# Stores of gated activations move from the SyncE queue to the ScalarE queue in a one-core diffusion layer

## Chip, cores and metric

One core of a Trainium2 chip runs the whole kernel. The metric is the device time of one execution in microseconds, the median of three runs. TensorE is called PE below, its weight loads PEld, VectorE DVE, ScalarE ACT, GpSimd POOL and SyncE SP, as in the profile.

## What is computed

One layer of a hybrid backbone over 1024 latent tokens and 256 context tokens, width 1024, all in 32-bit floats:

```python
x   = x   + 0.5 * m2  * swiglu(modulate(rmsnorm(x),   m0,  m1),  w_ffn1_in, w_ffn1_out)
ctx = ctx + 0.5 * mc2 * swiglu(modulate(rmsnorm(ctx), mc0, mc1), w_ffn1_in, w_ffn1_out)
# one projection to q, k, v and the gates of a short convolution; latent queries
# attend to latent and context keys; both halves are joined
x   = x + m5 * (concat(rmsnorm(a), rmsnorm(s)) @ w_mix_out)
x   = x + 0.5 * m8 * swiglu(modulate(rmsnorm(x), m6, m7), w_ffn2_in, w_ffn2_out)
return rmsnorm(x)

def swiglu(h, w_in, w_out):              # hidden width 2816, 22 blocks of 128
    gate, up = split(h @ w_in, 2)
    return (silu(gate) * up) @ w_out
```

## The kernel before

Activations lie transposed, 128 features on the partitions, and latent tokens come in two halves of 512 columns (`L0`, `L1`); the context block is `CX` with 256. Every matrix product is made of three matmuls, from a high and a low part of both operands: `split` (L308) makes them by a cast on ACT and a subtraction on DVE (L309, L310).

Each SwiGLU is an object of class `FFN`. Its 22 hidden blocks ("units" below, index `f`) pass through two stages.

**First stage** (`phase_a`, L512, units 2 to 21; units 0 and 1 are made by plain products in the head). Latent tokens and output columns are each taken in two halves, and the 2x2 block product is made with seven products instead of eight, of 12 matmuls each. In time order they are M1, M6, M2, M5, M7, M4, M3; the first SwiGLU has two products for the context in between (cG, cU). ACT copies M1's bank out (`e1`, L528), after which M2 adds into the same bank, so M2's first matmul waits for that copy. ACT takes SiLU of M2's result (L531) and of M3's (L559), DVE makes the other sums and the two gating multiplications (L549, L579). At the odd unit of each pair POOL makes sums of gated blocks (L552, L554), and at the end of every unit one more (L583 or L585): these are the operands of a second seven-product scheme that the output projection uses. All of them are stored to DRAM:

- `store` (L349): for an odd unit P3 (the product of L549), P7 and P6 (POOL's sums of L552 and L554), then P2 (L579) and P4 (POOL, L583); for an even unit P1 (L579) and P5 (POOL, L585). That is seven stores of 256 KB in a pair of units.
- `spill` (L353) passes latent blocks on to `store`, and stores the context's gated block (128 KB, first SwiGLU only).

`prep` makes the weight operands of the next unit from raw tiles: `gA`, `S`, `sA`, `sB`, `uA`. At the end of a unit `load` (L460) asks for the raw tiles of unit `f+2` (L464, L465; three buffers with the tag `raw`, which the modulation weights share in the first SwiGLU). In that SwiGLU the modulation vectors are also computed beside the products (`ada_steps`, with a cast L152 on ACT and a subtraction L153 on DVE ahead of small matmuls L155, L156).

**Second stage** (`phase_b`, L670): steps named after `KINDS`, `P1` to `P4`, each of six blocks. `prep_b` loads the stored sums (`grt`, L651) and weights (`wr`, `res`, L614), splits them (`gst`, `wo`), and matmuls of L704 to L706 add into four banks, which L667 takes out. `pair0` (L361) loads four gated blocks of units 0 and 1 back, makes POOL's sums of them and stores these too.

**Order.** Each engine runs its own queue in order; an instruction at the head that waits holds everything behind it. The framework fixes each queue's order when the program is built: it keeps a model of when operands are ready, and gives an engine the earliest instruction of the program among those that it holds to be ready. All DMAs are issued from SP's queue, so loads and stores stand in one line there. Eight counters for landed DMAs are used in rotation, and a DMA waits until the one eight before it has landed.

Of the kernel before, what the change touches and what calls it, by code (L numbers as in the profile page):

```python
# [27 lines left out]
def layer_kernel(  # L28
# [18 lines left out]
    pe, act, dve, sp = nc.tensor, nc.scalar, nc.vector, nc.sync  # L47
# [286 lines left out]
    class FFN:  # L334
# [13 lines left out]

        def store(self, kind, p, t):  # L349
            p = (p - 1) % (NF // 2)  # L350
            sp.dma_start(self.gq[kind][p // 2][:, p % 2, :], t)

        def spill(self, f, b, t):  # L353
            if b is CX:
                sp.dma_start(self.gc[self.fs[f] // 2][:, self.fs[f] % 2, :], t)
            elif b is L0 and f % 2 == 0:
                sp.dma_start(self.g12, t)
            else:
                self.store("P3" if b is L0 else ("P1", "P2")[f % 2], f // 2, t)
# [661 lines left out]
    def side_b1(k, i):  # L1021
# [17 lines left out]
        elif k in ("P1", "P6", "P7"):  # L1039
            if k == "P1" and i == 0:  # L1040
                nc1[0] = norm_mod_steps(CX, 1, t2("rcx", [P, 256]))
            adv(nc1[0])
            if k == "P7" and i == 5:
                run(nc1[0])
                ctx_kv()
        elif k == "P4":
            if i == 0:
                nc1[0] = norm_mod_steps(L0, 1)
            adv(nc1[0], 2)
            if i == 5:  # L1050
                run(nc1[0])
                spill(L0, 0)

    F1.phase_b(side_b1)
    norm_mod(L1, 1)
    spill(L1, 1)


# [776 lines left out]
```

## Time and profile before

| What | Value |
|---|---|
| median of 3 runs | 2164.17 us (2163.52 to 2165.6) |
| time of the profiled execution | 2168.2 us |
| its span, first to last instruction | 2166.4 us |
| mean granted TensorE clock | 0.995 of full speed |
| first SwiGLU, first stage with its modulation work | about 111 to 636 us |
| second SwiGLU, first stage | about 1530 to 1922 us |
| second SwiGLU, second stage | about 1917 us to the end |

Busy time is the time in which an engine ran instructions; matmul ends are modelled and overlap, so the distance between starts tells PE's pace. A row of a timeline gives start, duration, engine (a q behind it: the queue itself, for issued DMAs), line, operation and tiles, and in brackets how long the engine was idle before it and what ended that. DMA issues are not part of an engine's busy time.

### The profile page before, as it was taken

How to read it: one execution, taken by the hardware profiler on the slowest of the kernel's cores; microseconds unless marked ns; L12 is line 12 of the kernel's file. 1: busy time of each engine (PE TensorE's matmuls, PEld its weight loads, DVE VectorE, ACT ScalarE, POOL GpSimd, SP SyncE). 2: the span in 40 equal slices, each digit the busy share in tenths (PEclk: the TensorE clock that was granted, in tenths of full speed). 3: DMA queues.
4: the chain of work that ended last, by engine and by line, in shares of the span. 5: the costliest groups of instructions: out<-in, count | busy, mean ns of one | idle time of the engine just before them, and what ended most of it. 6: DMA issues, size and time to landing. Idle time of an engine off the chain costs nothing.

```text
span 2166.4 us, 26536 instructions
## 1 busy us (share of the span) xinstructions
PE 2130.6 (98%) x10084; PEld 1711.8 (79%) x10084; DVE 1546.3 (71%) x2109; ACT 910.1 (42%) x1415; POOL 227.6 (11%) x158
## 2 busy tenths in 40 slices
PE   8999999999999999999999999999999999999998
PEld 4788788888889887887777777777788888877877
DVE  5887776666657867661898899876866666668754
ACT  4422322222335533442567777754422232234433
POOL 0001111101010110000100100001011111123001
PEclk9999999999999999999999999999999999999998
DMA  8043344545379756342211101142232322378642
GB/s 323 16 146 127 124 147 138 167 130 170 127 242 341 263 178 228 119 136 68 88 49 30 40 20 68 49 151 73 78 99 101 117 94 91 107 287 283 225 147 78
DMA packets 111824, 296.01 MB, mean 137 GB/s; under 512 B 10704, under 2 KB 17872, under 8 KB 108624
## 3 DMA queue, kind: packets, MB, share of 16 engines
q1 hardware_dynamic: 111696, 294.32, 40.1%
q8 instruction: 79, 1.29, 0.2%
q14 instruction: 49, 0.40, 0.1%
HBM read 235.29 MB, written 56.36 MB: 135 GB/s over the span
## 4 chain that ended last, share of the span: by engine, by line
PE 75%; DVE 6%; DMA 4%; issue 2%; ACT 2%; POOL 0%; DVEq 0%; SPq 0%; ACTq 0%; POOLq 0%
PE p L508 9%; PE p L510 9%; PE p L509 9%; PE po L704 6%; PE po L706 6%; PE po L705 6%; DMA wa<-in_ada_dram 3%; PE pT L1331 1%; PE pT L1330 1%; PE pmo L1110 1%; PE pmo L1111 1%; PE pmo L1112 1%; PE pvo L1354 1%; PE pvo L1355 1%; PE pvo L1353 1%
## 5 line engine op out<-in xcount | busy, mean ns | idle before, releaser
L704 PE MATMUL po<-gst,wo 128*128 128x512 f32 (+1 forms) x636 | 248.4, 391 | 3.4 <-DVE x L667 3.4
L706 PE MATMUL po<-gst,wo 128*128 128x512 f32 (+1 forms) x636 | 247.2, 389 | 4.0 <-DVE wo L310 4.0
L705 PE MATMUL po<-gst,wo 128*128 128x512 f32 (+1 forms) x636 | 247.3, 389 | 0.0
L309 ACT CAST gst<-grt 128x1024 fp32r<-128x1024 f32 (+1 forms) x95 | 88.9, 936 | 218.7 <-PE po L706 96.4
L310 DVE TENSOR_TENSOR gst<-grt,gst 128x1024 fp32r<-128x1024 f32 (+1 forms) x95 | 110.6, 1165 | 73.7 <-ACT gst L309 73.5
L706 PEld LDWEIGHTS po<-gst,wo 128*128 128x128 f32 x636 | 120.0, 189 | 31.9 <-DVE wo L310 5.1
L704 PEld LDWEIGHTS po<-gst,wo 128*128 128x128 f32 x636 | 120.1, 189 | 31.5 <-issue 2.7
L705 PEld LDWEIGHTS po<-gst,wo 128*128 128x128 f32 x636 | 120.2, 189 | 26.4
L142 DVE SCALAR_TENSOR_TENSOR acc<-wa,cs,acc 128x1024 f32<-128x1024 f32 x70 | 90.5, 1314 | 60.3 <-DMA wa<-in_ada_dram 60.3
L508 PE MATMUL p<-h0h,wgA 128*128 128x512 f32 x320 | 126.6, 396 | 0.2 <-ACT e1f L528 0.2
L509 PE MATMUL p<-h0l,wgA 128*128 128x512 f32 x320 | 126.4, 395 | 0.0
L510 PE MATMUL p<-h0h,wgA 128*128 128x512 f32 x320 | 126.4, 395 | 0.0
L1333 ACT ACTIVATE pexp<-pT 128x512 f32<-128x512 f32 x160 | 94.5, 598 | 66.6 <-PE pT L1331 35.1
L309 ACT CAST wsB<-s 128x512 fp32r<-128x512 f32 x80 | 48.5, 620 | 152.9 <-DVE s L495 83.0
L277 DVE TENSOR_TENSOR wm<-wr,wm 128x1024 fp32r<-128x1024 f32 x52 | 64.8, 1249 | 42.3 <-ACT wm L273 42.0
L310 DVE TENSOR_TENSOR wo<-wr,wo 128x1024 fp32r<-128x1024 f32 x72 | 83.3, 1163 | 15.2 <-ACT wo L309 15.2
L310 DVE TENSOR_TENSOR wsA<-s,wsA 128x512 fp32r<-128x512 f32 x80 | 51.8, 687 | 54.3 <-ACT wsA L309 54.3
L309 ACT CAST wo<-wr 128x1024 fp32r<-128x1024 f32 x72 | 70.3, 976 | 27.2 <-DVE wr L628 16.1
L309 ACT CAST wuA<-wr 128x1024 fp32r<-128x1024 f32 (+1 forms) x40 | 33.5, 838 | 107.6 <-issue 58.7
L309 ACT CAST wsA<-s 128x512 fp32r<-128x512 f32 x80 | 45.6, 618 | 68.9 <-PE p L510 63.1
L508 PEld LDWEIGHTS p<-h0h,wgA 128*128 128x128 f32 x320 | 60.1, 188 | 14.6 <-ACT e1f L528 0.6
L510 PEld LDWEIGHTS p<-h0h,wgA 128*128 128x128 f32 x320 | 60.1, 188 | 14.5
(1077 smaller groups left out, 5966.8 us busy)
## 6 DMA issues: line engine op xcount, KB each, us to landing
wr<-in_wo_dram SPq DMA_DIRECT2D x92, 512.0 KB, 4.7
wr<-in_wi_dram SPq DMA_DIRECT2D x88, 512.0 KB, 3.7
wa<-in_ada_dram SPq DMA_DIRECT2D x56, 512.0 KB, 3.6
wr<-in_wmi_dram SPq DMA_DIRECT2D x38, 512.0 KB, 3.6
grt<-g1P SPq DMA_DIRECT2D x35, 512.0 KB, 4.8
grt<-g2P SPq DMA_DIRECT2D x35, 512.0 KB, 6.0
g1P<-ev SPq DMA_DIRECT2D x35, 256.0 KB, 3.2
g2P<-ev SPq DMA_DIRECT2D x35, 256.0 KB, 2.0
```

What stands on the lines that cost most here:

```text
L142: dve.scalar_tensor_tensor(acc[:, i, :], w, cs[:, j, k:k + 1], acc[:, i, :], op0=ALU.mult, op1=ALU.add)
L277: dve.tensor_tensor(w[:, 1, :], r, w[:, 0, :].bitcast(F32), op=ALU.subtract)
L309: act.copy(hi, t)
L310: dve.tensor_tensor(lo, t, hi.bitcast(F32), op=ALU.subtract)
L508: pe.matmul(pt, w[:, 0, c:c + P], hi, start=(k == 0 and not more), stop=False, skip_group_check=more)
L509: pe.matmul(pt, w[:, 0, c:c + P], lo, start=False, stop=False, skip_group_check=more)
L510: pe.matmul(pt, w[:, 1, c:c + P], hi, start=False, stop=(k == 3), skip_group_check=more)
L704: pe.matmul(o, wh, hi, start=st, stop=False, skip_group_check=g)
L705: pe.matmul(o, wh, lo, start=False, stop=False, skip_group_check=g)
L706: pe.matmul(o, wl, hi, start=False, stop=end, skip_group_check=g)
L1110: pe.matmul(pt, wh, hi[:, k, :], start=(i == 0), stop=False)
L1333: act.activation(p, pt, AF.Exp)
```

## The change

`store` and the context branch of `spill` issue their DMA from ACT's queue instead of SP's. Nothing else is edited: the store of the first L0 block (`g12`), all loads, spills of the residual and output stores stay on SP. The framework makes the order of all queues anew.

```diff
         def store(self, kind, p, t):
             p = (p - 1) % (NF // 2)
-            sp.dma_start(self.gq[kind][p // 2][:, p % 2, :], t)
+            act.dma_start(self.gq[kind][p // 2][:, p % 2, :], t)
 
         def spill(self, f, b, t):
             if b is CX:
-                sp.dma_start(self.gc[self.fs[f] // 2][:, self.fs[f] % 2, :], t)
+                act.dma_start(self.gc[self.fs[f] // 2][:, self.fs[f] % 2, :], t)
```

## Rows read from the trace of the kernel before

**Rows 1.** The page, part 1: busy us (share of span) of each engine
```profile
PE 2130.6 (98%) x10084; PEld 1711.8 (79%) x10084; DVE 1546.3 (71%) x2109; ACT 910.1 (42%) x1415; POOL 227.6 (11%) x158
```
**Rows 2.** Busy time by stretches: second SwiGLU's first stage, then its second stage's start
```profile
1770.00:1905.00 135.00, 135.00 (x581) 108.94 (x581) 88.34 (x117) 39.61 (x63) 19.74 (x13) 1.00 0.29 100
1905.00:1960.00 55.00, 52.17 (x221) 40.90 (x220) 37.52 (x36) 16.54 (x18) 11.65 (x8) 1.00 0.91 329
```
**Rows 3.** PE's waits, 100 to 640 us: total, times, longest
```profile
PE pr L156 <- DVE alo L153: 2.1, 3, 0.8
...
PE p L508 <- ACT e1f L528: 0.2, 1, 0.2
```
**Rows 4.** PE's waits, 1525 to 1905 us
```profile
PE p L510 <- DVE wsA L310: 1.0, 1, 1.0
```
**Rows 5.** PE's waits, 1905 to 2000 us
```profile
PE po L706 <- DVE wo L310: 1.9, 2, 1.3
PE po L704 <- DVE x L667: 1.5, 2, 0.9
```
**Rows 6.** The stores of line L351: engine, op, count, duration ns min/median/max
```profile
L351 SPq DMA_DIRECT2D g2P<-ev x35: 319/320/339, 1567.2 to 1926.6; - x35
...
L351 SPq DMA_DIRECT2D g1P<-e1f x15: 319/327/1040, 137.6 to 630.1; - x15
```
**Rows 7.** Timeline of SP's queue, 1720 to 1734 us (an odd unit)
```profile
1723.70 2.08 SPq L351 DMA_DIRECT2D g2P<-ev  x2
1726.84 0.32 SPq L351 DMA_DIRECT2D g2P<-e1f  x1
1727.25 0.38 SPq L464 DMA_DIRECT2D wr<-in_wi_dram  x1
1728.53 0.32 SPq L351 DMA_DIRECT2D g2P<-ev  x1
1730.28 0.32 SPq L351 DMA_DIRECT2D g2P<-gt  x1
```
**Rows 8.** Timeline of SP's queue, 1701 to 1712 us (the even unit before it)
```profile
1704.73 0.33 SPq L464 DMA_DIRECT2D wr<-in_wi_dram  x1
...
1709.70 0.33 SPq L351 DMA_DIRECT2D g2P<-gt  x1
```
**Rows 9.** Timeline of ACT, 1720 to 1734 us
```profile
1724.58 1.06 ACT L309 CAST wgA<-wr 128x1024 fp32r<-128x1024 f32 x1 [2.13 <-PE p L510]
1725.53 0.63 ACT L559 ACTIVATE ev<-ev 128x512 f32<-128x512 f32 x1
1727.55 0.59 ACT L528 COPY ev<-p 128x512 f32<-128x512 f32 x1 [1.39 <-DMA g2P<-ev]
1733.03 0.60 ACT L531 ACTIVATE e1f<-p 128x512 f32<-128x512 f32 x1 [4.89 <-PE p L510]
```
**Rows 10.** Timeline of POOL, 1720 to 1734 us
```profile
1725.51 1.31 POOL L554 TENSOR_TENSOR e1f<-ev,e1f 128x512 f32<-128x512 f32 x1
1728.63 1.62 POOL L583 TENSOR_TENSOR gt<-e1f,ev 128x512 f32<-128x512 f32 x1 [1.82 <-issue]
```
**Rows 11.** Timeline of PE, 1729 to 1731 us: M2's first matmul
```profile
1729.98 0.40 PE L508 MATMUL p<-h0h,wgA 128*128 128x512 f32 x1
```
**Rows 12.** Chain that ended last, 1900 to 2000 us: start, us, what
```profile
1928.87 0.32 SPq L351
1929.24 0.43 SPq L614
...
1936.31 6.83 DMA resc<-in_wo_dram
...
1944.38 1.22 DVE wo L310
```
**Rows 13.** Timeline of POOL, 1936 to 1950 us: the last sum of the first pair
```profile
1941.21 2.17 POOL L374 TENSOR_TENSOR g<-g,g 128x512 f32<-128x512 f32 x1
```
**Rows 14.** Timeline of ACT, 1936 to 1950 us
```profile
1939.74 1.06 ACT L309 CAST gst<-grt 128x1024 fp32r<-128x1024 f32 x1 [14.25 <-DMA grt<-g2P]
```

## The prediction, as put on record before the result was known

> **What bounds the kernel now.** I read the page first, then the busy time by stretches, then what PE waited for, and last SP, ACT, POOL and PE side by side over one pair of units. PE is busy for 98% of the span, ACT for 42% [rows 1]. In the second SwiGLU's first stage PE has no gap in 135 us: 581 matmuls, one per 0.232 us, at full granted clock, while ACT runs 39.6 us of these 135 and the DMA engines are busy 0.29 of the time [rows 2]. That stage is bound by PE alone, so whatever the stores do there can't make it faster; it can only make it slower. What the change can win is PE's waits near the stores. There are few. In the first SwiGLU's first stage the larger ones are 2.1 us for a subtraction of the modulation work, and 0.2 us for the copy of M1's bank [rows 3]. In the second SwiGLU's first stage there is one wait of 1.0 us, at its very start [rows 4]. Where the second stage begins there are 1.9 us for weight splits and 1.5 us for the taking out of banks [rows 5]. Together 6.7 us, which is 0.3% of the time: the ceiling of every gain.
>
> **What is moved, and its price on ACT.** Counted from the code: seven stores in each of ten pairs of units and in two SwiGLUs make 140; units 0 and 1 add three for each SwiGLU, `pair0` four for each, the context 22. That is 176 stores. On SP an issue takes 0.32 us, the longest 1.04 [rows 6]. The trace shows no DMA on ACT, so these are the bounds there; I take 0.33, since a median of the same instruction is the nearest row. It is added work, so it can't be below nothing. 176 x 0.33 = 58 us on an engine with 2166 - 910 = 1256 us idle [rows 1]: hidden as long as no instruction behind a store has PE waiting for it.
>
> **Who has PE waiting.** One instruction of ACT does, in every unit: the copy L528 of M1's bank, for M2 adds into that bank. In the odd unit shown it runs from 1727.55 to 1728.14 [rows 9], and M2's first matmul starts at 1729.98 [rows 11]: 1.84 us to spare. The weight casts (`wgA` and the like) are made a whole unit, 84 x 0.232 = 19.5 us, ahead of use, and SiLU L531 comes 5.5 us after the copy. So up to 1.8 us of delay ahead of L528 is free, and each further microsecond costs one.
>
> **What the stores put ahead of it.** They wait for their data at the head of the queue. In the odd unit, SP issued P3 at 1723.70, P7 at 1723.70 + 2.08 - 0.32 = 1725.46, P6 at 1726.84, P2 at 1728.53 and P4 at 1730.28 [rows 7]; P6 comes as POOL's second sum ends at 1726.82, and P4 as its third ends at 1730.25 [rows 10]. The order of ACT's new queue isn't in the trace, but one row tells what the builder does with stores: the load L464, which in the even unit was issued at 1704.73 [rows 8], would have been due one unit later at about 1724.3, and stands behind P3, P7 and P6, at 1727.25 [rows 7]. So the builder thinks POOL's sums are ready earlier than they are, and lets them go first. I assume the same on ACT: P3, P7, P6, then SiLU L559, the cast `wgA`, and L528. Worked out: P6 leaves ACT at 1726.84 + 0.33 = 1727.17, L559 takes 0.63 (1727.80), `wgA` 1.06 (1728.86), L528 0.59 (1729.45) [rows 9]. That is 0.5 us ahead of M2 at 1729.98 [rows 11]. With P2 ahead of L528 as well (0.33 more) it is 0.2 us ahead. Cost: nothing, but most of the cover is used. Behind L528 there is none to hurry until L531 at 1733.03 [rows 9], by which P2 and P4 have long gone. In the first SwiGLU two context products lie around these steps; the one tight copy there is late already by 0.2 us [rows 3]. A store just ahead of each of these four waits [rows 3] would cost 4 x 0.33 = 1.3 us; that is the upper bound, nothing the lower, and I take nothing, since casts and copies there mostly stand in idle stretches of ACT.
>
> **What it frees on SP.** In the first stages a raw tile asked for at 1704.73 [rows 8] is cast at 1724.58 [rows 9], so 3 us more or less [rows 7] are worth nothing. At the end of the second SwiGLU's first stage they are. The chain that ended last runs there through the store P4, issued at 1928.87, the load right behind it at 1929.24, a load that lands after 1943, and the split `wo` at 1944.38, for which PE waits [rows 12]. With P3 to P4 gone from SP's queue these loads can leave up to 6 us earlier. Gain: nothing at the least (the stretch moves 329 GB/s with the DMA engines busy 0.91 of the time [rows 2], so an earlier start may only lengthen the transfers); all 3.4 us of [rows 5] at the most; I take 1.3, the longest of those waits, as it is the one to which this chain leads. [...]
>
> **`pair0`.** Its four stores wait for POOL's sums, the last until 1943.38 [rows 13]. On ACT they pass the casts of that stretch, the first of them at 1939.74 [rows 14]. If the builder puts them ahead of that cast they hold it for up to 1943.38 + 0.33 - 1939.74 = 3.97 us, and PE with it; if behind, nothing. I take nothing: on SP they stood behind loads for the steps that these casts serve. In the first SwiGLU the same four lie beside context steps without a PE wait.
>
> **The sum.** ACT's issues 0, copies 0, loads -1.3, `pair0` 0: -1.3 us on the profiled execution's own 2168.2 us (span 2166.4). The median of the runs, 2164.17, lies 4.0 us below that execution; the same step from it gives 2162.9 us.
>
> **The rivals.**
> - *A store waits for POOL ahead of the copy* (slower). If the builder puts P4 ahead of the next unit's L528, the copy starts at 1730.28 + 0.33 = 1730.61 and ends at 1731.20, 1.22 us after M2 was due [rows 7, 9, 11]. This decides as soon as P4 stands ahead of L528, wherever the rest stands. Nine odd units of the second SwiGLU have such a copy behind them: 11.0 us. In even units P5 is issued at 1709.70 [rows 8], the copy would end at 1710.62, and M2 is due at 1729.98 - 19.5 = 1710.5: 0.1 us each, 1 us for ten. So 12 us in the second SwiGLU; with as much in the first, 24. For it: the builder already hurries POOL's sums, and P4 stands earlier in the program than L528. Against it: P4 comes 2.7 us after the copy's start, more than the 1.3 to 1.6 us of one POOL sum [rows 10] by which the builder may be wrong. Time: 2164.2 + 12 = 2176 (to 2188 with both).
> - *Loads freed everywhere* (faster). All 6.7 us of PE's waits go: 2157.5. For it: the wait for `alo` hangs on modulation loads in the same queue. Against it: [rows 3, 4] name ACT and DVE, not a DMA, as what ended these waits.
> - *It does nothing*: the loads are held by the landing of earlier ones, and ACT hides the issues: 2164.2.
> - *The issue on ACT is dearer.* At 1.04 us [rows 6] P6 leaves ACT at 1727.88, and the copy ends at 1727.88 + 0.63 + 1.06 + 0.59 = 1730.16, 0.2 us late, nine times: +2 us. [...]
>
> **How the numbers follow.** A difference of 0.2% (4.3 us) is about what a measurement of this kernel can tell from no change. My forecast together with "does nothing" and "dearer issue": 0.56, from 2160.8 (all of [rows 5] won) to 2167.5. The store ahead of the copy: 0.32, from 2170 to 2188. Loads freed everywhere: 0.12. So faster 0.12, same 0.56, slower 0.32. The likeliest case gives 2162.9. The range starts at 2159.5, a little beyond the bound of 2160.8, and ends at 2178, where the first form of the slower rival is in and the second, with some 0.1 of the chance, is left out.
>
> **What would show it.** Right: ACT's queue shows 0.3 us issues, L528 in the odd units moves from 1.4 us of idle time to directly behind `wgA`, and M2 follows M1 and M6 without a gap; SP's loads of the second stage's start leave some 5 us earlier and the wait for `wo` is gone. Wrong, slower side: PE waits for "ACT L528" about nine times at 1.2 us, and ACT waits for POOL's `gt` ahead of L528. Wrong, faster side: the waits of [rows 3] are gone. If PE's waits change in stages that hold no store, such as attention, then it is the new order of the queues as a whole that moved the time, which none of these sums covers.

## The result, and the profile after

The changed kernel takes 2195.0 us (median of 4 runs, 2192.67 to 2196.87) beside 2164.89 us for the kernel before on the same chip: a ratio of 1.0133, interval 1.0119 to 1.0147. It is slower by 30 us, above the upper end of the forecast range. The profiled execution took 2192.67 us with a span of 2190.9 us, against 2166.4 us before: 24.5 us more. The other 5.6 us lie between the medians and the profiled executions, which took 3.3 us more than the median before and 2.3 us less after.

By the starts of matmuls, these 24.5 us divide as follows (microseconds). The first SwiGLU's first stage is counted to the first matmul of its context steps, its second stage to its last matmul; the second SwiGLU's first stage is counted to its own last matmul, and the rest of the second stage from there to its last.

| Stage | before | after | difference |
|---|---|---|---|
| first SwiGLU, first stage | 524.8 | 531.1 | +6.3 |
| first SwiGLU, context steps and second stage | 287.6 | 293.2 | +5.6 |
| attention and what lies around it | 607.1 | 606.3 | -0.8 |
| second SwiGLU, first stage | 394.2 | 407.8 | +13.6 |
| second SwiGLU, rest of the second stage | 233.5 | 233.0 | -0.5 |

One trace gives such a stage to within some 3 us only: the last row, 233.5 us before, was 236.7 us in the run with only the first SwiGLU's last two units on ACT, whose second SwiGLU stores from SP as before, and where the granted clock stood at 0.50 twice more, for 3.4 us each.

ACT's busy time hardly changed, since issues don't count in it, and PE stayed busy for 98% of a longer span [rows 1]. The page of the changed kernel, part 1:

```profile
PE 2136.7 (98%) x10084; PEld 1714.3 (78%) x10084; DVE 1528.0 (70%) x2109; ACT 908.2 (41%) x1415; POOL 222.6 (10%) x158
```

The same 135 us of the second SwiGLU's first stage by stretches (start:end, length, then busy time and instructions of PE, PEld, DVE, ACT and POOL, clock, DMA share, GB/s): 561 matmuls where there were 581 [rows 2], at full clock.

```profile
1770.00:1905.00 135.00, 131.19 (x561) 105.08 (x560) 81.93 (x113) 37.42 (x60) 18.95 (x13) 1.00 0.27 92
```

PE's waits in that stage, 1540 to 1935 us. Before, there was the last of these lines alone, with 1.0 us [rows 4]:

```profile
PE p L508 <- ACT ev L528: 6.4, 5, 1.3
PE p L508 <- ACT e1f L528: 5.1, 4, 1.3
PE p L510 <- DVE wsA L310: 1.5, 1, 1.5
```

Nine waits of 1.3 us for the copy L528, one behind each odd unit with a successor: the picture that the slower rival asked for. The timeline of ACT over one of them, 1741 to 1753 us, answers [rows 9]:

```profile
1741.66 2.09 ACTq L351 DMA_DIRECT2D g2P<-ev  x2
1744.81 0.33 ACTq L351 DMA_DIRECT2D g2P<-e1f  x1
1745.18 0.63 ACT L559 ACTIVATE ev<-ev 128x512 f32<-128x512 f32 x1 [4.78 <-POOL e1f L554]
1745.71 1.04 ACT L309 CAST wgA<-wr 128x1024 fp32r<-128x1024 f32 x1
1746.57 0.33 ACTq L351 DMA_DIRECT2D g2P<-ev  x1
1748.32 0.33 ACTq L351 DMA_DIRECT2D g2P<-gt  x1
1748.74 0.58 ACT L528 COPY ev<-p 128x512 f32<-128x512 f32 x1 [1.99 <-POOL gt L583]
1752.48 0.60 ACT L531 ACTIVATE e1f<-p 128x512 f32<-128x512 f32 x1 [3.16 <-PE p L510]
```

POOL's sum and PE's first matmul of M2 at the same place, from their timelines:

```profile
1746.67 1.62 POOL L583 TENSOR_TENSOR gt<-e1f,ev 128x512 f32<-128x512 f32 x1 [1.90 <-issue]
```

```profile
1749.38 0.50 PE L508 MATMUL p<-h0h,wgA 128*128 128x512 f32 x1 [1.29 <-ACT ev L528]
```

Read from the bottom: M2 waits for the copy, the copy stands behind the store P4 (`gt`) in ACT's queue, and P4 stands at its head until POOL's sum ends at 1748.29. M1's last matmul had started at 1744.90, so the copy's data had long been there. M2 starts 1.44 us later after M1 than it does behind an even unit; 9 x 1.44 = 13.0 us, and 0.5 us more at the stage's start (1.5 for `wsA` instead of 1.0) makes 13.5 of the 13.6 us. Behind an even unit the copy stands ahead of the store P5: in the unit before it ends at 1726.36, and M2 starts at 1728.37, 2.0 us later.

### The profile page after: what moved, and what is told of

It reads as the page before. It is cut to its first block, busy times and chain, and to the rows that moved or that the text cites. A ratio compares the mean times of both kernels' runs of the same rounds, so it can differ in the third digit from the quotient of the medians.

```text
span 2190.9 us, 26509 instructions
## 1 busy us (share of the span) xinstructions
PE 2136.7 (98%) x10084; PEld 1714.3 (78%) x10084; DVE 1528.0 (70%) x2109; ACT 908.2 (41%) x1415; POOL 222.6 (10%) x158
## 3 DMA queue, kind: packets, MB, share of 16 engines
q8 instruction: 79, 1.29, 0.2%
```

## The experiments

The runs of a group shared their runs of the kernel before; "ratio" is time over theirs, with its 95% interval. Stage times are from the traces, counted as in the table above. In these kernels `store` takes a queue as a last argument `q`; where a diff doesn't show that line, a store without it goes to ACT.

**P4 alone back on SP.**

```diff
-                        self.store("P4" if h else "P5", pi, t)
+                        self.store("P4" if h else "P5", pi, t, sp if h else act)
```

> The changed kernel with one store moved back: the odd units' P4 is issued from SP again, all others stay on ACT. Theory (P4 waits for POOL at the head of ACT's queue, ahead of the copy L528 for which M2 waits): the nine gaps of about 1.27 us of PE in the second SwiGLU's first stage go, that stage falls from 407.8 us to between 394 and 396, and the first SwiGLU's first stage, where few P4 stand ahead of a copy, from 531.1 to between 526 and 530; the second stages stay. Time 2195.0 - 12.6 - (1 to 5) = 2177 to 2182. Rival (it is the number of issues on ACT, or the new order of all queues, and not this one wait): the second SwiGLU's first stage stays above 404 us, and the time between 2190 and 2196.

2177.0 us, ratio 1.0054 (1.0039 to 1.0068). The second SwiGLU's first stage took 394.1 us, 0.1 less than before the change, without one wait for L528; the first SwiGLU's 527.3. One of the seven kinds of store carries the 13 us, although 20 of 176 issues left ACT.

**`pair0` alone back on SP.**

```diff
             for k, v in (("P5", t1), ("P7", b12), ("P6", b11), ("P4", b21)):
-                self.store(k, 0, v)
+                self.store(k, 0, v, sp)
```

> The changed kernel with the four stores of pair0 moved back to SP in both SwiGLUs. Theory (the 5.6 us that the first SwiGLU's second stage lost come from pair0's stores, which wait for POOL ahead of the casts of gst and wo on ACT): that stage falls from 231.8 us to about 226, the PE gap of 3.4 us at its start is gone, the clock there stays at its full level, the first stages keep 531 and 408 us; time about 2189. Rival (the loss comes from the order in which the loads and the last units' P4 stand, pair0 has no part in it): the stage stays at 231 to 232 us and the time at 2194 to 2196.

2191.1 us, ratio 1.0118 (1.0102 to 1.0135). The theory fell: context steps and second stage of the first SwiGLU still took 292.5 us (293.2 with the full change). The interval overlaps that of the full change (1.0119 to 1.0147), so the times alone don't show that `pair0` cost anything. The traces show a wait that went, where the second SwiGLU's second stage begins. PE's waits were, in the full change (1930 to 2025 us):

```profile
PE po L704 <- DVE x L667: 2.4, 1, 2.4
```

and with `pair0` on SP (1929 to 2025 us):

```profile
PE po L704 <- DVE x L667: 0.3, 1, 0.3
```

The wait of 2.4 us was followed by 3.4 us at a granted clock of 0.50, from 1979.1 us, which the run with `pair0` on SP does not have there. Both traces still took 640.8 us for the second SwiGLU's two stages as counted above: at the end of the second run the clock stood at 0.50 for 3.4 us twice more than in the full change.

The chain that ended last in the full change, 1944 to 1985 us, tells what the wait hung on (start, us, what):

```profile
1962.25 6.16 DMA g2P<-g
1968.43 5.15 DMA grt<-g2P
1973.68 1.06 ACT gst L309
1978.26 0.67 DVE x L667
1979.07 0.72 PE po L704
```

The first line is a store of `pair0`, issued by ACT. It landed at 1968.41, and SP issued the load `grt` 0.02 us later: both have the same one of the eight counters, and the load comes next on it after the store. Of this trace's 669 DMAs none was issued before the one ahead of it on its counter had landed. The load brings other blocks than those that `pair0` stores. The other three stores of `pair0` each held one of SP's issues in the same way (1963.67, 1967.20 and 1970.31, within 0.06 us of the landing); in the kernel before and in the run with `pair0` on SP no issue followed one of them so closely. So stores that had left SP's queue still held SP's issues here.

**P4, P5 and `pair0` back on SP**, the edits of both runs together, and P5 as well.

```diff
-                        self.store("P4" if h else "P5", pi, t)
+                        self.store("P4" if h else "P5", pi, t, sp)
```

> The changed kernel with P4, P5 and pair0 moved back to SP; P1, P2, P3, P7, P6 and the context's blocks stay on ACT, 104 issues. Theory (only stores that wait for POOL ahead of a copy or a cast cost): first stages at about 525 and 395 us, first SwiGLU's second stage at 226 to 227, second SwiGLU's second stage keeps its small gain; time 2164 to 2169. Rival (each issue on ACT costs a share of the 30 us): 104 of 176 issues are left, so 2195 - 30 x 72/176 = 2183.

2173.4 us, ratio 1.0038 (1.0023 to 1.0053), between the two expectations. The first stages took 525.4 and 395.0 us, as the theory said; the first SwiGLU's context and second stage stayed at 295.1.

**All on ACT, P4 behind the copy.** P4 is issued in the program after the next unit's SiLU of M2 (`pair0` from SP).

```diff
-                        self.store("P4" if h else "P5", pi, t)
+                        if h and f < NF - 1:
+                            late = pi, t
+                        else:
+                            self.store("P4" if h else "P5", pi, t)
...
                         act.activation(e2, p1, AF.Silu)
+                        if h == 0 and f > f0:
+                            self.store("P4", *late)
```

> The changed kernel with P4 still on ACT, but written in the program behind the next unit's SiLU of M2, so that it stands behind the copy L528 in ACT's queue; pair0 from SP. The number of issues on ACT is that of the changed kernel less eight. Theory (the place in the queue decides, not the engine or the number of issues): second SwiGLU's first stage 394 to 396 us, first SwiGLU's 526 to 530, time 2165 to 2176. Rival (ACT can't carry these issues, wherever they stand): second SwiGLU's first stage over 404 us, time over 2188.

2173.3 us, ratio 1.0035 (1.0017 to 1.0052); the second SwiGLU's first stage took 394.0 us. ACT at an odd unit, 1730 to 1740 us of this kernel:

```profile
1734.52 1.03 ACT L309 CAST wgA<-wr 128x1024 fp32r<-128x1024 f32 x1
1735.37 0.33 ACTq L351 DMA_DIRECT2D g2P<-ev  x1
1735.80 0.59 ACT L528 COPY ev<-p 128x512 f32<-128x512 f32 x1 [0.25 <-DMA g2P<-ev]
1737.12 0.33 ACTq L351 DMA_DIRECT2D g2P<-gt  x1
```

The copy ends at 1736.39, and M2 starts without a wait at 1736.74: 0.35 us to spare. This is the order that the prediction had assumed, with P2 ahead of the copy, for which it had worked out 0.2 us.

**Five kinds of store in the second SwiGLU only, and four of them.**

```diff
-            sp.dma_start(self.gq[kind][p // 2][:, p % 2, :], t)
+            (q or (act if self.which in (2,) and kind in ('P3', 'P7', 'P6', 'P2', 'P4') else sp)).dma_start(self.gq[kind][p // 2][:, p % 2, :], t)
```

> The kernel before, with only the second SwiGLU's odd-unit stores P3, P7, P6, P2 and P4 issued from ACT: 50 issues instead of 176; the first SwiGLU, P1, P5 and pair0 are untouched. In ACT's queue P2 and P4 stand ahead of the copy L528. Theory (P4 at the head of ACT's queue waits for POOL and holds the copy): the second SwiGLU's first stage is 407 to 409 us, as with all 176 issues; its second stage 234 to 237; the first SwiGLU as before. Time 2164.2 + 13 - (1 to 3) = 2174 to 2177. Rival (the loss grows with the number of issues): 13.6 x 50/70 = 9.7 us and less than 404 us for the stage; or none, if the even units' P5 did it: 394.

> As the run with five stores, but P2, which DVE makes and which waits for no POOL sum, is issued from SP again. P4 stays on ACT; with one issue less ahead of it the builder puts it behind the copy L528. Theory (only the place of P4 against the copy counts): the second SwiGLU's first stage falls to 394 to 395 us, no PE wait for L528 is left, and the time is 2160 to 2164. Rival (P4 on ACT costs in itself, or P2 has a price of its own of 0.3 us in ten units): 404 us and more, or 394 + 3.

With five: 2178.0 us, ratio 1.0059 (1.0041 to 1.0077), the stage 407.9 us, as long as with all the stores. With four, P2 being the one left out: 2164.5 us, ratio 0.9993 (0.9981 to 1.0005), the stage 393.8 us. PE's waits with five, 1540 to 1905 us (with four there is none):

```profile
PE p L508 <- ACT ev L528: 6.4, 5, 1.3
PE p L508 <- ACT e1f L528: 5.1, 4, 1.3
```

P4 is on ACT in both. With four it stands behind the copy (timeline of ACT, 1715 to 1730 us):

```profile
1726.80 0.59 ACT L528 COPY ev<-p 128x512 f32<-128x512 f32 x1
1728.25 0.33 ACTq L351 DMA_DIRECT2D g2P<-gt  x1
```

One store, which waits for no POOL sum, changes where the builder puts P4, and that is worth 14 us. P2 itself ahead of the copy costs nothing: it stands there in the runs with P4 on SP and with P4 late as well, where the stage took 394.1 and 394.0 us.

**All kinds in the second SwiGLU only, P4 late**: the edit of the fourth run, with `act if self.which else sp` in `store`.

> All stores of the second SwiGLU's first stage from ACT, with P4 written in the program behind the next unit's SiLU of M2, so that it stands behind the copy; pair0 and the whole first SwiGLU from SP as in the kernel before. Theory (the gain of the freed SP queue is confined to the second SwiGLU's second stage, 2.5 to 3.4 us there when neither P4 nor pair0 holds ACT, against 1.2 in the changed kernel): first stage 394, second stage 234 to 235.5, time 2160.5 to 2162. Rival (the gain came from the changed first SwiGLU and is not here): 2164.

2162.3 us, ratio 0.9985 (0.9976 to 0.9995): a little faster than the kernel before. Of the waits of [rows 5] 0.3 us was left. The second stage, which the expectation counts from its own first matmul, took 236.6 us against 237.8, where 234 to 235.5 was expected; the trace shows why. After the wait of 2.1 us for `wo` near the end, which both kernels have, the granted clock stood at 0.50 for 3.4 us twice before the last matmul, and in the kernel before not at all. Up to that wait the rest of the second stage took 214.9 us against 218.7.

**Only the last pair of units of the second SwiGLU.**

```diff
-            sp.dma_start(self.gq[kind][p // 2][:, p % 2, :], t)
+            (q or (act if self.which == 2 and self.tail else sp)).dma_start(self.gq[kind][p // 2][:, p % 2, :], t)
...
+                self.tail = f >= NF - 2
                 pi, h = divmod(f, 2)
```

> The kernel before, with only the seven stores of the last pair of units of the second SwiGLU issued from ACT; pair0 and all else from SP. No copy L528 follows the last P4. Theory (the gain of the change is that the loads of the second stage no longer stand behind stores that wait for POOL, at this one place): second SwiGLU's first stage 394, its second stage 234 to 236 us against 237.8, time 2161 to 2163. Rival (the gain needs a queue free of stores through the whole first stage, for loads made early): second stage 237.5 to 238, time 2164 to 2165.

2163.1 us, ratio 0.9981 (0.9971 to 0.9991), the lowest ratio of all, with seven stores moved (its interval overlaps that of the run before). The second stage took 231.5 us from its first matmul against 237.8, more gain than the 2 to 4 us expected; 3.4 us less at a clock of 0.50, some 1.7 us, are part of it. PE's waits from 1905 us to the end; the kernel before had 4.0, 2.6 and 0.6 us under these names:

```profile
PE po L708 <- DVE wo L310: 2.1, 1, 2.1
PE po L706 <- DVE x L669: 1.1, 2, 0.8
PE rb L211 <- DVE rs L204: 0.6, 1, 0.6
```

**What cost 5.6 us in the first SwiGLU's second stage.** PE's waits came to 5.3 us against 1.7; some 1.7 us more are the clock, which fell after the longest (see the last section). The waits in the full change, 640 to 930 us; the kernel before had the second and third line alone (0.9 and 0.8 us):

```profile
PE po L704 <- DVE x_c L667: 3.4, 1, 3.4
PE pv L292 <- ACT wv L273: 0.9, 1, 0.9
PE po L704 <- DVE x L667: 0.7, 1, 0.7
PE po L704 <- DVE rs L204: 0.3, 1, 0.3
```

In DVE's queue the taking out of the context's banks (`x_c`) stands behind weight subtractions that wait for loads. The timeline of DVE in the full change, 704 to 711 us (before, that line ran at 694.72, as the context steps ended; here they ended at 700.50):

```profile
704.59 1.22 DVE L310 TENSOR_TENSOR wo<-wr,wo 128x1024 fp32r<-128x1024 f32 x1
706.33 1.23 DVE L626 TENSOR_TENSOR res<-wr,res 128x1024 f32<-128x1024 f32 x1 [0.53 <-DMA res<-in_wo_dram]
707.47 3.22 DVE L667 SCALAR_TENSOR_TENSOR x_c<-po,mod,x_c 128x256 f32<-128x256 f32 x8
```

Two things had changed besides: SP issued three of the four 1 MB loads of the residual `x` ahead of the context steps instead of one (a second came 0.8 us after their start), and DVE's queue had two more subtractions L628 ahead of the reciprocal `rs`. Three runs, each built on the one with P4, P5 and `pair0` on SP, took these apart: two loads of `x` held, three held, and, with three held, the two subtractions on POOL. The first diff is of the run with two held, the second of the last.

```diff
             if i in (12, 16):
+                g = F1.pg[i][:, 0, 0:1].bitcast(F32)
+                pool.tensor_tensor(L1.x[i // 16][:, 0, 0:1], g, g, op=ALU.add)
                 half_x(L1, xt_d, 512, i // 16)
...
-                dve.tensor_tensor(r, r, R, op=ALU.subtract)
+                e = pool if k == "P6" and u >= 4 and self.cx else dve
+                e.tensor_tensor(r, r, R, op=ALU.subtract)
```

> As the run with P4, P5 and pair0 on SP, with one thing more: the last two 1 MB loads of the residual x in the first SwiGLU are held back until the context steps 12 and 16 (a one-column addition on POOL writes into their target first), so that they stand again where the kernel before issued them, some 28 and 39 us after the first context step, instead of one of them 4 us ahead of it. Theory (SP, freed of the stores, issues this 1 MB ahead of the weight blocks of wo, the DMA engines are busy for over 0.9 of the time there, and the blocks, the DVE work on them and the taking out of the context's banks behind it come late): context stage and second stage together fall from 295.2 us to 288 to 290, the 3.1 us wait for x_c is below 1 us, time about 2167. Rival (DVE's queue has the taking out of the banks behind later subtractions, whenever the blocks land): together still over 293 us, time 2172 to 2174.

> As the run with P4, P5 and pair0 on SP, with the last three of the four 1 MB loads of the residual x in the first SwiGLU held back until the context steps 8, 12 and 16 (the run before this held two). The freed SP queue then takes three loads of res, needed at the start of the second stage, in their place. Theory (1 MB blocks of x that are needed only after 730 us, issued ahead of blocks of wo, make DVE's subtractions on those blocks late, and the taking out of banks and the context's norm stand behind these on DVE): with x held and res early, the waits for x_c and for rs both go, context stage and second stage together 287 to 289 us (before: 287.7), time about 2165 to 2168. Rival (the loads are late because weights and stored sums are asked for later by the changed order, x has no part in what is left): the wait of 2 to 3 us for rs stays, together 291 to 293 us.

> As the run with three loads of x held, and with two subtractions of the first SwiGLU's step P6 (L628, those for resb and resc) made by POOL instead of DVE. In DVE's queue the taking out of P1's first bank and the reciprocal rs then stand again where the kernel before had them, with no instruction ahead of them that waits for the late weight blocks. Theory (what is left of the loss in the first SwiGLU's second stage is a place in a queue too: DVE's new order has two subtractions that wait for a load ahead of the reciprocal for which PE waits): the 3.0 us wait for rs falls below 0.5 us, context stage and second stage together from 292.5 us to 288 to 289.5, time about 2167 to 2170. Rival (the weight blocks themselves come late, and PE waits for them, whoever subtracts): the wait moves to another name, wo or gst, and the two stages stay at 291.5 us or more.

Context steps and second stage took 291.5, 292.4 and 293.2 us (ratios 1.0045, 1.0046 and 1.0033, each within 0.0017). Holding `x` took the wait for `x_c` from 3.1 us to 0.5 and to none, but 3.0 us for `rs` stayed in both, and the stages stayed above the 288 to 290 and the 287 to 289 us that the theory had expected; with the subtractions on POOL there were 2.2 and 1.2 us again, and the loads came some 3 us later in that execution. None of the three carries the loss alone.

So the next two runs moved the boundary as a whole, from both sides: the run with P4, P5 and `pair0` on SP with the first SwiGLU's last two units on SP too, and the kernel before with only these two units' nine stores on ACT.

```diff
-            (q or act).dma_start(self.gq[kind][p // 2][:, p % 2, :], t)
+            (q or (sp if self.which == 0 and self.tail else act)).dma_start(self.gq[kind][p // 2][:, p % 2, :], t)
```

```diff
-            sp.dma_start(self.gq[kind][p // 2][:, p % 2, :], t)
+            (q or (act if self.which == 0 and self.tail else sp)).dma_start(self.gq[kind][p // 2][:, p % 2, :], t)
```

(`tail` as above, and the context's store in `spill` likewise.)

> As the run with P4, P5 and pair0 on SP, with the first SwiGLU's last two units moved back to SP too: seven stores and the two context blocks. The builder then gives SP's loads of x and DVE's queue at the start of the first SwiGLU's second stage the order of the kernel before. Theory (that stage's loss hangs on the order that the queues get at this one boundary, not on the stores of the stage as a whole): context stage and second stage together 287.5 to 288.5 us, against 295.2; the waits for x_c and rs are gone; time 2163 to 2168. Rival (it hangs on the other stores on ACT, or on their wait for POOL): together 291 us or more.

> The kernel before, with only the first SwiGLU's last two units on ACT: seven stores and the two context blocks; the second SwiGLU, pair0 and all else from SP. It is the mirror of the run before. Theory (the order at the boundary): the first stage keeps its 524 us, context stage and second stage together rise from 287.7 to between 291 and 295 us, with PE waits for x_c or rs of 3 to 5.4 us; time 2168 to 2173. Rival (nine stores more or less on ACT change nothing here): 288 us, time 2164 to 2167.

The first: 287.7 us for the two stages, ratio 1.0004 (0.9994 to 1.0013). The second: 294.8 us, ratio 1.0019 (1.0009 to 1.0029). PE's waits, 640 to 930 us, with the last two units on SP:

```profile
PE po L704 <- DVE x L667: 0.9, 1, 0.9
PE pv L292 <- ACT wv L273: 0.9, 1, 0.9
```

and with only these two on ACT:

```profile
PE po L704 <- DVE rs L204: 3.3, 1, 3.3
PE po L704 <- DVE x_c L667: 2.1, 1, 2.1
```

Three more waits there, of 0.8 to 0.9 us, are left out. Nine stores at the boundary carry the whole loss of this stage, whatever the other stores do. With them gone from SP's queue the builder fills it with later loads and orders DVE's queue as if those had landed. How much of it is the loads and how much DVE's order stays open. So does a third candidate, which no run tested: in the full change SP's issues at 643.74, 645.24, 647.45 and 649.94 us came within 0.06 us of the landing of the DMA eight before on their counter, which was three times a store from ACT and once a 1 MB load of `x`. In the kernel before two issues at this place did (642.49 and 643.12).

## Why the prediction was wrong, point by point

- **What bounds the kernel: right.** PE alone bounds the second SwiGLU's first stage (no gap in 135 us [rows 2]), and there the change could only cost. The ceiling of 6.7 us left out waits of 0.9 us each for L544 and L152 in the first SwiGLU and of 3.2 us for `wo` and `x` after 2000 us; the largest gain found, about 4 us, stayed below it all the same.
- **The issue's price on ACT: right.** 0.326 us at the median of all 176, as on SP; the longest took 0.487 us (two groups of L351 on ACT in the full change: count, then ns min/median/max):

```profile
L351 ACTq DMA_DIRECT2D g1P<-gt x20: 326/326/327, 139.3 to 646.5; - x20
L351 ACTq DMA_DIRECT2D g2P<-e1f x15: 326/326/487, 1563.2 to 1948.7; - x15
```

  The dearer issue of the rival, 1.04 us by [rows 6], did not come with two issuers.
- **Who has PE waiting, and the sums behind it: right.** With P4 behind the copy the spare time was 0.35 us, forecast 0.2. With P4 ahead of it the wait was 1.29 us, forecast 1.22.
- **The order of ACT's queue: the step that failed.** The prediction put P4 behind L528, since P4 comes 2.7 us after the copy's start and the builder was taken to err by one POOL sum, 1.3 to 1.6 us. The runs showed P4 ahead of L528 and nine waits of 1.3 us. The rows that it had used itself spoke against so small an error: the load L464, due at 1724.3, was put behind P6, whose data came at 1726.82 [rows 7, 8, 10], so the builder had erred by 2.5 us or more about POOL's sums, close to the 2.7. And the run with four kinds shows that the place hangs on one store more or less ahead of it. By these rows the slower rival deserved a larger chance. Its price, 11.0 us for nine odd units, came to 13.0; its 1 us for even units to nothing, since P5 was put behind the copy there.
- **The first SwiGLU's first stage: taken at nothing (bound 1.3 us), cost 6.3 us.** The slower rival had allowed 12 us for it. PE's waits for the copy there (100 to 640 us; 0.2 us before [rows 3]) in the full change:

```profile
PE pr L156 <- DVE alo L153: 3.0, 3, 1.5
PE p L508 <- ACT ev L528: 2.9, 2, 1.6
PE pr L155 <- ACT ahi L152: 2.3, 4, 1.0
PE p L508 <- ACT e1f L528: 1.3, 2, 0.8
```

  The copy takes 4.0 us of it, the modulation's casts and subtractions some 2 us more. The two waits for `ev`, 2.9 us, have a `gt` that waits for POOL ahead of the copy (at 275.83 a P4, at 564.06 a P5); the two for `e1f` have casts and L559 there. With P4 alone back on SP the stage took 3.8 us less. Kernels whose first SwiGLU wasn't touched took 522.3 to 524.8 us in this stage, so differences of 2 to 3 us between single traces don't count, and which store costs what here stays open.
- **The loads freed at the second stage: right in kind, too small.** The load of `res` was issued at 1929.24, after the first stage's last matmul (1921.58), and in the full change at 1942.93, before it (1946.50): 11 us earlier by the stage, where up to 6 were forecast. The 1.9 us of waits for `wo` [rows 5] went; forecast 1.3. In the run without `pair0` on ACT all but 0.3 of the 3.4 us of [rows 5] went; in the full change `pair0` put a wait of 2.4 us in their place. Moving the stores saved time here (ratio 0.9981 with seven of them moved): what was saved is the time that loads stood behind stores whose data was not there, as the load of 1929.24 stood behind P4 of 1928.87 [rows 12].
- **`pair0`: taken at nothing, and by another path than its bound.** The bound of 3.97 us had its stores hold a cast on ACT. In the trace the cast behind them, of `wo` at 1964.88, waited for a load that landed at 1964.86, and PE's wait hung on the load that stood behind a store's counter. The wait grew by 2.1 us (2.4 against 0.3), and the clock after it took some 1.7 us by the estimate of the last section; the times of whole runs don't tell this from nothing. In the first SwiGLU the run without it shows nothing.
- **The first SwiGLU's second stage: no term at all, cost 5.6 us.** The prediction had named only attention as a place where a new order of the queues would show. The new order of SP's and DVE's queues, which the sum left out, moved the time here, and P4's place in ACT's queue moved it in the second SwiGLU's first stage.

## What to carry to other kernels

A DMA issue on ACT was cheap here (0.33 us), but it waited at the head of ACT's queue for its data, as P4 did for POOL's sum until 1748.29 us, and nine such waits cost PE 1.3 us each. Before moving an issue, list what stands behind it and who waits for that, and read the built order of the queues, which is fixed before any run, rather than argue it. Move the few transfers that stand ahead of something urgent (seven stores gave all the gain that was found, 0.2%), keep those that wait for a slow producer (here a sum of 1.62 us on POOL) off an engine that feeds TensorE, or write them behind the urgent instruction. A queue that is freed gets filled by the builder with other work: in the first SwiGLU's context steps and second stage, where that happened, 5.6 us were lost. Two queues that share the counters for landed DMAs are not apart: four issues of SP waited here for the landing of a store from ACT and left within 0.06 us of it. And read the granted clock before comparing one trace with another: two stretches of 3.4 us at 0.50 hid a gain here.

## What the runs showed of the hardware

In the full change the granted clock fell to 0.50 (from 709.4 to 712.8 us) just after a wait of PE of 3.4 us. No matmul started between 704.6 and 708.4 us; soon after it matmuls started 0.43 us apart instead of 0.23 (columns as above):

```profile
704.00:708.00 4.00, 0.97 (x5) 0.45 (x3) 3.48 (x5) 1.06 (x2) 0.00 (x0) 1.00 1.04 396
708.00:710.00 2.00, 1.60 (x6) 1.26 (x7) 2.00 (x6) 2.00 (x4) 0.00 (x0) 0.84 1.05 396
710.00:712.00 2.00, 2.00 (x6) 1.57 (x5) 2.00 (x4) 1.91 (x5) 0.00 (x0) 0.50 1.07 405
712.00:715.00 3.00, 3.00 (x13) 2.42 (x12) 3.00 (x4) 1.61 (x3) 0.00 (x0) 0.87 0.87 278
```

By an estimate from these rows that adds about 1.7 us (0.16 x 2 + 0.50 x 2 + 0.13 x 3) to a wait of 3.4 us. The nine waits of 1.3 us left the clock at 1.00. After the wait of 2.1 us for `wo` near the end it stayed at 1.00 in the full change and in the kernel before, and fell to 0.50 in the runs with `pair0` on SP and with all kinds in the second SwiGLU and P4 late.

In the run with two subtractions on POOL, a subtraction on DVE that took 1.22 us while POOL was idle took 2.77 us while POOL ran one of 2.53 us:

```profile
723.94 1.22 DVE L310 TENSOR_TENSOR gst<-grt,gst 128x1024 fp32r<-128x1024 f32 x1
...
726.87 2.77 DVE L310 TENSOR_TENSOR gst<-grt,gst 128x1024 fp32r<-128x1024 f32 x1
```

```profile
726.03 2.53 POOL L629 TENSOR_TENSOR wr<-wr,resb 128x1024 f32<-128x1024 f32 x1 [51.53 <-DMA wr<-in_wo_dram]
```
